# Three blocks of a gate projection written as seven-product blocks, with three engines kept in program order

## The chip, the cores and the metric

The kernel runs on one core of one Trainium2 chip. The metric is the time of one execution on the device in microseconds (us); a comparison takes the median of several runs. The engines of the core are TensorE (PE in the rows, with its weight load PEld), VectorE (DVE), ScalarE (ACT), GpSimd (POOL) and SyncE (SP), whose queue issues nearly all transfers.

## What is computed

One layer of a hybrid decoder: 512 tokens, width 1024, float32. A windowed attention (A) and a gated linear attention (B) run on the same normalised input `h`, and their projections are merged through two gates. Then follow a SwiGLU feed-forward part, a gated per-layer input and a final norm. The part that matters here:

```python
h = rms_norm(x, norm_mix)
proj = h @ w_in                       # q, k, v, ..., og, gate_a, gate_g side by side
o_g = rms_norm(o_g, gla_norm) * silu(og)
y_g = o_g @ w_proj_gla
mixed = sigmoid(gate_a) * y_a + sigmoid(gate_g) * y_g
x = x + mixed @ w_out
```

`gate_g = h @ w_in[:, 4880:5904]` is the merge gate of the linear attention: 1024 columns, worked on in four blocks of 256, called `gg0` to `gg3` in the kernel. The next matrix after it is `w_proj_gla`, the blocks `pg0` to `pg3`.

## The kernel before

**Arithmetic.** Every float32 operand of a large product is split into a high and a low part (`split`, L105): ScalarE casts the high part (L111), VectorE subtracts it from the source for the low part (L112). `mm3` (L121) then makes one float32 product out of three matmuls, high by high, high by low and low by high (L122 to L124). That is why each product stands under three lines in the rows.

**Two ways to make a block of 256 weight columns by 512 tokens.** The plain one is `fm_pair`: two halves of 128 columns (`e`), eight slices of the inner dimension, three matmuls each, every one 512 tokens wide: 48 matmuls. The other is `quad_pair`: the block is cut in two along columns, tokens and inner dimension, and sums of quarter blocks replace one of the eight quarter products, so there are seven. Each is four slices by three matmuls of 256 tokens: 84 matmuls. It needs sums of the tokens' side (`h_t1` to `h_t4`, made once and kept), and for each block two sums of the weights, made by `sums_to`: one VectorE operation of 128x1024 (`s0`) and two GpSimd operations of 128x512 (`s1`), all at L253. Its products run as follows: `pa`, `pb`, `pa` again, `pc`, `pa`, `pb`, `pa`. The bank `pa` accumulates over four of the seven, and after each of these ScalarE copies its present value out (`copy`, L580: `u` twice, `v`, then the second half of the result); the next product on `pa` has to wait for that copy. VectorE adds the other banks to the copies (`add`, L576). The kernel uses `quad_pair` for most of q/k (`qk1` to `qk3`), for the output gate `og0` to `og3` and for the whole feed-forward input (`fg..`, `fu..`).

**Weights.** `Weights` holds the order of all weight tiles. Raw weights come in by SyncE's queue (L243) into a ring of four half tiles, that is two whole ones (`RAW = 4`); the feed-forward weights have one whole tile more. One block of 256 columns fills one whole tile. The load for a block is issued when the block two before it has given its raw tile back: a plain block does that when both halves are split, a seven-product block after its last split (`.3`) and its sums. `take` splits two tiles ahead (`AHEAD = 2`) and makes sums up to `SUMS = 5` tiles ahead.

**Order.** Each engine executes its list strictly in the order of the built program, and SyncE issues its transfers likewise. The lists are made by a scheduler with priorities, except in sections under `tc.manual_schedule`, where the engines named there keep the order in which the code was written. Before the change such sections are the start of the kernel and the feed-forward part. Transfers that are not weights go through `aside` (L309), which puts them on SyncE's queue behind the last weight load that the code has asked for by then.

**Around the gate.** While `gg0` runs, the last head of the linear attention ends on the other engines (`lin`); its result goes to DRAM in eight pieces (`ogd`, L311). `og_splits` loads it back in two transfers of 1 MB (`ogr0` with rows 0 to 3, `ogr1` with rows 4 to 7) and splits each in two halves into `og_h`, `og_l`, the operand of `pg0`. The tanh of each gate block (L1080) goes to DRAM as `mgd` and comes back as `mg` when `pg` is evacuated. All of `gg1` to `gg3`, the splits of `ogr` and the weights of `pg` are in lists that the scheduler made.

Of the kernel before, what the change touches and what calls it, by code (L numbers as in the profile page):

```python
# [20 lines left out]
KD = D // P  # L21
# [7 lines left out]
C_GK, C_OG, C_GA, C_GG = 2816, 2832, 3856, 4880  # L29
# [4 lines left out]
def hybrid_layer(  # L34
# [26 lines left out]
    nc = tc.nc  # L61
# [18 lines left out]
    def tok(t):  # L80
        return slice(t * P, (t + 1) * P)

    def a8(name, shape=(P, 4, S), dt=F32):
        return big.tile(list(shape), dt, tag="a8", name=name)

    def t2(name, shape=(P, 512), dt=F32):
        return tp.tile(list(shape), dt, tag="t2", name=name)

    def bank(name):
        return psum.tile([P, 512], F32, tag="ps", name=name)  # L90
# [17 lines left out]
    def split(dst, src, scale=None, eng=nc.vector):  # L108
        hi, lo = dst
        if scale is None:  # L110
            ins = nc.scalar.copy(hi, src)  # L111
            eng.tensor_tensor(out=lo, in0=src, in1=hi.bitcast(F32), op=ALU.subtract)  # L112
        else:
            ins = nc.scalar.activation(hi, src, AF.Copy, scale=scale)  # L114
            nc.vector.scalar_tensor_tensor(  # L115
                out=lo, in0=src, scalar=scale, in1=hi.bitcast(F32), op0=ALU.mult, op1=ALU.subtract
            )
        return ins.ins

    def mm3(ps, l, r, first, last, more=False):  # L120
        kw = dict(skip_group_check=True) if more else {}  # L121
        nc.tensor.matmul(ps, lhsT=l[0], rhs=r[0], start=first, stop=False, **kw)  # L122
        nc.tensor.matmul(ps, lhsT=l[0], rhs=r[1], start=False, stop=False, **kw)  # L123
        nc.tensor.matmul(ps, lhsT=l[1], rhs=r[0], start=False, stop=last, **kw)  # L124


    wk = w_in.rearrange("(k p) c -> p k c", p=P)
# [10 lines left out]
    def u_quad(name, mat, c0):  # L138

        units.append((name, None, [[((ALL,), mat[:, 4 * kh : 4 * kh + 4, c0 : c0 + 256])] for kh in range(2)]))  # L140

    def u_rows(name, mat, k0, n, c0, ncol=512, per=2):

        for u in range(n // per):
            k = k0 + per * u
            units.append((f"{name}{u}", (per, ncol), [((ALL,), mat[:, k : k + per, c0 : c0 + ncol])]))
# [28 lines left out]
    for i in range(4):  # L175
# [5 lines left out]
                [((slice(64 * g, 64 * g + 64),), wpa[g][:, :, 256 * i : 256 * i + 256]) for g in range(2)],  # L181
            )
        )
    for i in range(4):
        u_rows(f"gg{i}", wk, 0, KD, C_GG + 256 * i, 256, 4)
    for i in range(4):
        u_rows(f"pg{i}", wpg, 0, KD, 256 * i, 256, 4)
    for i in range(2):
# [117 lines left out]
    W = Weights()  # L306

    def aside(dst, src):

        with tc.issue_after(W.dma.ins):  # L310
            nc.sync.dma_start(dst, src)  # L311
# [67 lines left out]
    for i in range(2):  # L379
        ps = bank(f"gm{i}")  # L380
# [25 lines left out]
    hT = HQuads("h")  # L406
# [63 lines left out]
    for t in range(NT):  # L470
        ps = bank(f"v0ps{t}")
# [73 lines left out]
    def fm_mms(ps, w, cols, rhs, k0, nk, first, last):  # L545
        for k in range(nk):
            mm3(ps, (w[0][:, k, cols], w[1][:, k, cols]), rhs.rows(k0 + k), first and k == 0, last and k == nk - 1)

    def flush(late, every=False):

        for job in late or []:
            job[0] -= 1
        while late and (every or min(late)[0] < 1):
            late.pop(late.index(min(late)))[2]()

    def quad_pair(name, act, c, evac, late=None):


        def done(e):
            if late is None:  # L560
                evac(e)
            else:
                late.extend(evac(e))

        pa, pb, pc = (bank(f"{name}p{x}") for x in "abc")
        H = (slice(0, 256), slice(256, 512))

        def product(ps, w, i, x, first=True):
            hi, lo = act.q(x)
            for k in range(4):  # L570
                mm3(ps, (w[0][:, i, k, :], w[1][:, i, k, :]), (hi[:, k, :], lo[:, k, :]), first and k == 0, k == 3, not first)


        def add(out, a, b):
            with tc.high_priority(offset=1000):
                nc.vector.tensor_tensor(out=out, in0=a, in1=b, op=ALU.add)  # L576

        def copy(out, a):
            with tc.high_priority(offset=1000):
                nc.scalar.copy(out, a)  # L580


        part = t2(f"{name}u"), t2(f"{name}v")
        p1, u2, u3, u4 = (part[i // 2][:, H[i % 2]] for i in range(4))
        run = pa[:, H[0]]
        w = W.take(f"{name}.0")
        product(run, w, 0, "b11")
        copy(p1, run)
        flush(late)
        product(pb[:, H[0]], w, 1, "b21")  # L590
        add(c[0][:, H[0]], pb[:, H[0]], p1)
        yield
        w = W.take(f"{name}.1")
        product(run, w, 0, "t2", False)
        copy(u2, run)
        flush(late)
        product(pc[:, H[0]], w, 1, "b22")
        add(u4, pc[:, H[0]], u2)
        yield
        w = W.take(f"{name}.2")  # L600
        product(run, w, 0, "t3", False)
        copy(u3, run)
        flush(late)
        product(pb[:, H[1]], w, 1, "t1")
        add(c[0][:, H[1]], pb[:, H[1]], u4)
        done(0)
        add(c[1][:, H[1]], pb[:, H[1]], u3)
        yield
        w = W.take(f"{name}.3")
        product(run, w, 0, "t4", False)  # L610
        copy(c[1][:, H[0]], run)
        flush(late)
        done(1)
        yield

    def fm_pair(name, act, evac):

        pss = [bank(f"{name}p{x}") for x in "ab"]
        for kh in range(2):
            w = W.take(f"{name}{kh}")  # L620
            for e in range(2):
                fm_mms(pss[e], w, tok(e), act, 4 * kh, 4, kh == 0, kh == 1)
                if kh:
                    evac(e, pss[e])
                yield

    def drive(stream, other=None, rate=1):
        for _ in stream:
            if other is not None:
                for _ in range(rate):  # L630
                    next(other, None)
# [4 lines left out]
    ps = bank("bias_ps")  # L636
# [411 lines left out]
    def times_gate(out, t, y, eng=nc.vector):  # L1048
        eng.scalar_tensor_tensor(out=out, in0=t, scalar=1.0, in1=y, op0=ALU.add, op1=ALU.mult)
# [22 lines left out]

    mx = Split("mx")

    def gates_g():
        for i in range(4):
            c = [t2(f"sgg{i}{e}") for e in range(2)]

            def evac(e, ps):
                nc.scalar.activation(c[e], ps, AF.Tanh, scale=0.5)  # L1080
                aside(mgd[i, 1, e], c[e])

            yield from fm_pair(f"gg{i}", hT, evac)

    def og_splits():
        for i in range(2):
            o = a8(f"ogr{i}")
            aside(o, ogd[4 * i : 4 * i + 4].rearrange("k p t -> p k t"))
            for h in range(2):
                ks_ = slice(2 * h, 2 * h + 2)  # L1090
                split(ogT.part(i, ks_, ALL), o[:, ks_, :])
                yield

    gg = gates_g()
    for _ in range(4):
        next(gg)
        next(lin, None)
    for _ in lin:
        pass
    ogT = Split("og")  # L1100
    ogs = og_splits()
    drive(gg, ogs)
    for _ in ogs:
        pass
    for i in range(4):
        mg = a8(f"mg{i}", (P, 2, 2, 512))
        for m in range(2):
# [1 line left out]
        c = [t2(f"yg{i}{e}") for e in range(2)]  # L1109

        def evac(e, ps):
            times_gate(c[e], mg[:, 1, e], ps)
            nc.vector.tensor_tensor(out=c[e], in0=c[e], in1=mg[:, 0, e], op=ALU.add)
            split(mx.rows(2 * i + e), c[e])
# [153 lines left out]
    for gi, (f0, nf) in enumerate(FFN):  # L1268
        act = Split(f"act{gi}", nf)

        def inner():
            for i in range(nf // 2):
                gs = [t2(f"g{gi}{i}{e}") for e in range(2)]
                us = []

                def silu(e, gs=gs):
                    yield [1, next(jobs), lambda: nc.scalar.activation(gs[e], gs[e], AF.Silu)]

                def mult(e, i=i, gs=gs, us=us):
                    yield [  # L1280
                        1 + e,
                        next(jobs),
                        lambda: nc.vector.tensor_tensor(out=us[e], in0=us[e], in1=gs[e], op=ALU.mult),  # L1283
                    ]
                    yield [3, next(jobs), lambda: split(act.rows(2 * i + e), us[e])]

                yield from quad_pair(f"fg{gi}{i}", h2.hT, gs, silu, late)
                us += [t2(f"u{gi}{i}{e}") for e in range(2)]
                yield from quad_pair(f"fu{gi}{i}", h2.hT, us, mult, late)
# [8 lines left out]
        stream, late, jobs = inner(), [], count()  # L1298
# [117 lines left out]
```

## Time and profile before

| | |
|---|---|
| time, median of 3 runs | 871.7 us (871.03 to 872.21) |
| the profiled execution: time | 872.2 us |
| the profiled execution: span of the core | 870.4 us |
| TensorE busy in the span | 854.0 us, 98% |
| VectorE / ScalarE / GpSimd busy | 565.7 / 446.2 / 160.8 us |
| mean granted TensorE clock | 0.998 of full speed |
| `gg1`, first matmul, to `pg0`, first matmul | 332.84 to 365.48 us |

Times inside the kernel are us from the start of the span. The profiled execution is 0.5 us above the median of the runs and its span 1.8 us shorter than its time. Starts of matmuls are recorded; their ends are modelled, so distances between starts are what counts on TensorE.

### The profile page before, as it was taken

What the parts mean: (1) busy time and instruction counts of PE and PEld (TensorE: products, weight loads), DVE (VectorE), ACT (ScalarE), POOL (GpSimd) and SP (SyncE); (2) the same over time, 40 slices, a digit from 0 to 9 for tenths busy, and PEclk for the clock granted to TensorE, in tenths of its full rate; (3) what the DMA queues carried; (4) which work ended last, traced back from release to release, by engine and by line L of the source; (5) the groups of instructions that cost most, each with busy time, mean ns of one, the idle gap of its engine ahead of it and who ended that gap; (6) DMA issues with size and microseconds to landing.
All of it is one profiled execution on the core that took longest, in us unless ns stands there. A gap on an engine that the chain in (4) does not pass through costs nothing. (4 is left out here: it accounts for less than half of the span.)

```text
span 870.4 us, 14739 instructions
## 1 busy us (share of the span) xinstructions
PE 854.0 (98%) x5901; PEld 748.7 (86%) x5901; DVE 565.7 (65%) x821; ACT 446.2 (51%) x859; POOL 160.8 (18%) x149
## 2 busy tenths in 40 slices
PE   8999989999999999999999999999999999999996
PEld 7977878888777788888887999889999889998886
DVE  5533866769876643356368799635998437985574
ACT  6336587866755543333256556413565314554453
POOL 4340434120221110100011222011232012210101
PEclk9999999999999999999999999999999999999999
DMA  9382423133764256774415233611316311422502
GB/s 282 103 215 78 152 74 97 50 102 102 236 206 158 74 170 216 271 265 146 142 54 164 94 126 108 232 49 49 95 52 211 129 49 49 136 87 94 194 1 98
DMA packets 88245, 113.29 MB, mean 130 GB/s; under 512 B 6152, under 2 KB 64304, under 8 KB 87792
## 3 DMA queue, kind: packets, MB, share of 16 engines
q1 hardware_dynamic: 86704, 107.43, 38.2%
q0 software_dynamic: 1456, 4.92, 1.6%
q8 instruction: 46, 0.75, 0.4%
q14 instruction: 23, 0.19, 0.1%
q10 hardware_dynamic: 16, 0.00, 0.0%
HBM read 95.35 MB, written 15.93 MB: 128 GB/s over the span
## 5 line engine op out<-in xcount | busy, mean ns | idle before, releaser
L111 ACT CAST fo_h<-raw 128x1024 fp32r<-128x1024 f32 x22 | 22.5, 1050 | 30.5 <-PE fo00ps L124 13.1
L112 DVE TENSOR_TENSOR fo_l<-raw,fo_h 128x1024 fp32r<-128x1024 f32 x22 | 26.3, 1220 | 12.1 <-ACT fo_h L111 12.1
L326 POOL TENSOR_TENSOR or<-om,mhalf 128x1 f32<-128x1 f32 x16 | 14.2, 886 | 68.1 <-DVE om L330 54.2
L112 DVE TENSOR_TENSOR act_l<-u,act_h 128x512 fp32r<-128x512 f32 x22 | 22.1, 1004 | 5.4 <-ACT act_h L111 5.4
L905 DVE TENSOR_TENSOR zs<-zs,kq 128x512 f32<-128x512 f32 x28 | 19.5, 707 | 7.0 <-ACT zs L901 6.3
L112 DVE TENSOR_TENSOR pg_l<-raw,pg_h 128x1024 fp32r<-128x1024 f32 x8 | 9.8, 1223 | 18.5 <-ACT pg_h L111 18.5
L112 DVE TENSOR_TENSOR wo_l<-raw,wo_h 128x1024 fp32r<-128x1024 f32 x8 | 9.8, 1224 | 17.7 <-ACT wo_h L111 17.7
L115 DVE SCALAR_TENSOR_TENSOR gt_l<-raw,gple,gt_h 128x256 fp32r<-128x256 f32 (+1 forms) x24 | 12.9, 570 | 12.0 <-ACT gt_h L114 11.9
L114 ACT ACTIVATE gt_h<-raw,gple 128x256 fp32r<-128x256 f32 (+1 forms) x24 | 12.6, 573 | 12.4 <-PE gt0ps L124 8.1
L111 ACT CAST act_h<-u 128x512 fp32r<-128x512 f32 x22 | 13.7, 622 | 10.0 <-DVE u L1283 10.0
L111 ACT CAST wo_h<-raw 128x1024 fp32r<-128x1024 f32 x8 | 8.4, 1053 | 20.1 <-PE wo0ps L124 6.6
L112 DVE TENSOR_TENSOR gg_l<-raw,gg_h 128x1024 fp32r<-128x1024 f32 x8 | 9.8, 1224 | 12.9 <-ACT gg_h L111 12.9
L899 DVE TENSOR_TENSOR zs<-G 128x512 f32<-128x512 f32 x24 | 16.1, 692 | 2.4 <-DMA G<-Gd 2.4
L111 ACT CAST pg_h<-raw 128x1024 fp32r<-128x1024 f32 x8 | 8.4, 1055 | 15.7 <-PE gg3pb L123 5.8
L112 DVE TENSOR_TENSOR v_l<-raw,v_h 128x1024 fp32r<-128x1024 f32 (+1 forms) x8 | 9.3, 1167 | 11.1 <-ACT v_h L111 11.1
L997 ACT ACTIVATE own<-o,or 128x256 f32<-128x256 f32 x16 | 7.6, 475 | 17.1 <-POOL or L326 16.9
L1283 DVE TENSOR_TENSOR u<-u,g 128x512 f32<-128x512 f32 x22 | 16.1, 733 | 0.0
L111 ACT CAST v_h<-raw 128x1024 fp32r<-128x1024 f32 (+1 forms) x10 | 9.6, 973 | 11.9 <-PE v2ps L124 4.5
L792 ACT ACTIVATE s_all<-s_all,nm 128x256 f32<-128x256 f32 (+1 forms) x32 | 15.2, 480 | 0.7 <-DVE nm L789 0.7
L112 POOL TENSOR_TENSOR qa<-qa,qs 64x768 fp32r<-64x768 f32 x2 | 7.2, 3616 | 41.6 <-ACT qs L111 41.5
L111 ACT CAST gg_h<-raw 128x1024 fp32r<-128x1024 f32 x8 | 8.4, 1049 | 12.2 <-PE ga3pb L123 4.2
L112 DVE TENSOR_TENSOR qa_l<-raw,qa_h 128x512 fp32r<-128x512 f32 x8 | 5.5, 719 | 13.2 <-ACT qa_h L111 13.2
(2312 smaller groups left out, 3550.1 us busy)
## 6 DMA issues: line engine op xcount, KB each, us to landing
raw<-in_w_ffn_in SPq DMA_DIRECT2D x44, 512.0 KB, 4.7
raw<-in_w_in SPq DMA_DIRECT2D x39, 512.0 KB, 4.7
raw<-in_w_ffn_out SPq DMA_DIRECT2D x22, 512.0 KB, 4.8
raw<-in_w_proj_gla SPq DMA_DIRECT2D x8, 512.0 KB, 5.7
mg<-mgd SPq DMA_DIRECT2D x8, 512.0 KB, 7.0
raw<-in_w_out SPq DMA_DIRECT2D x8, 512.0 KB, 4.5
raw<-in_w_ple_gate SPq DMA_DIRECT2D x8, 512.0 KB, 4.3
raw<-in_w_in SPq DMA_DIRECT2D x8, 256.0 KB, 5.0
```

The costliest lines, as they stand in the source:

```text
L111: ins = nc.scalar.copy(hi, src)
L112: eng.tensor_tensor(out=lo, in0=src, in1=hi.bitcast(F32), op=ALU.subtract)
L114: ins = nc.scalar.activation(hi, src, AF.Copy, scale=scale)
L115: nc.vector.scalar_tensor_tensor(out=lo, in0=src, scalar=scale, in1=hi.bitcast(F32), op0=ALU.mult, op1=ALU.subtract)
L326: return r, nc.gpsimd.tensor_tensor(out=r, in0=a, in1=mhalf, op=ALU.pow)
L792: nc.scalar.activation(s[:, a, :], s[:, a, :], AF.Exp, bias=nm[:, a : a + 1], accum_out=su[:, a : a + 1])
L899: pe.tensor_tensor(out=z3, in0=g3, in1=g3[:, :, b - 1 : b].broadcast_to([P, nb, 2 * b]), op=ALU.subtract)
L905: nc.vector.tensor_tensor(out=d4, in0=d4, in1=kq_, op=ALU.mult)
L997: nc.scalar.activation(v_[:, c, :], po[:, 0:256], AF.Copy, scale=r)
L1283: lambda: nc.vector.tensor_tensor(out=us[e], in0=us[e], in1=gs[e], op=ALU.mult),
```

## The change

`gg1`, `gg2` and `gg3` become seven-product blocks; `gg0` stays plain. Their tanh is made in place on the finished tile, as a job that is put off by one product (`late`, `flush`). The rest of the stage, from the first product of `gg1` on, stands under `manual_schedule` for ScalarE, VectorE and GpSimd, with six places written by hand for `og_splits`: load `ogr0` after step 0, its two splits after steps 3 and 5, load `ogr1` after step 6, its splits after steps 9 and 11 (a block has four steps). TensorE's and SyncE's lists are still the scheduler's. `SUMS` is 4 in the section.

```diff
-    for i in range(4):
-        u_rows(f"gg{i}", wk, 0, KD, C_GG + 256 * i, 256, 4)
+    u_rows("gg0", wk, 0, KD, C_GG, 256, 4)
+    for i in range(1, 4):
+        u_quad(f"gg{i}", wk, C_GG + 256 * i)
...
+    late, jobs = [], count()
+
     def gates_g():
         for i in range(4):
             c = [t2(f"sgg{i}{e}") for e in range(2)]
 
-            def evac(e, ps):
+            def evac(e, ps, c=c, i=i):
                 nc.scalar.activation(c[e], ps, AF.Tanh, scale=0.5)
                 aside(mgd[i, 1, e], c[e])
 
-            yield from fm_pair(f"gg{i}", hT, evac)
+            def tanh(e, c=c, evac=evac):
+                yield [1, next(jobs), lambda: evac(e, c[e])]
+
+            if i:
+                yield from quad_pair(f"gg{i}", hT, c, tanh, late)
+            else:
+                yield from fm_pair(f"gg{i}", hT, evac)
...
             aside(o, ogd[4 * i : 4 * i + 4].rearrange("k p t -> p k t"))
+            yield
             for h in range(2):
...
-    drive(gg, ogs)
-    for _ in ogs:
-        pass
+
+    W.SUMS = 4
+    with tc.manual_schedule(engines={nc.scalar.engine, nc.vector.engine, nc.gpsimd.engine}):
+        for n, _ in enumerate(gg):
+            if n in (0, 3, 5, 6, 9, 11):
+                next(ogs)
+        flush(late, True)
+    W.SUMS = 5
```

SyncE's list from the last weights of the gate to the loads for `pg` (`raw25` is the whole tile of `gg3`, `raw26` of `pg0`, `raw27` of `pg1`, each loaded in two halves). Before:

```order
L243 DMA raw25_3613<-in_w_in 128x4x256 x2
L311 DMA mgd_1971<-sgg00_3605 128x512
L311 DMA ogd_1967<-og6_3673 128x512
L311 DMA ogd_1967<-og7_3681 128x512
L311 DMA mgd_1971<-sgg01_3606 128x512
L243 DMA raw26_3710<-in_w_proj_gla 128x4x256
L311 DMA ogr0_3724<-ogd_1967 128x4x512
L243 DMA raw26_3710<-in_w_proj_gla 128x4x256
L311 DMA mgd_1971<-sgg10_3702 128x512
L311 DMA ogr1_3761<-ogd_1967 128x4x512
L311 DMA mgd_1971<-sgg11_3703 128x512
L243 DMA raw27_3789<-in_w_proj_gla 128x4x256 x2
```

The same stretch of SyncE's list after the change:

```order
L244 DMA raw25_3618<-in_w_in 128x4x256
L312 DMA mgd_1971<-sgg00_3610 128x512
L312 DMA ogd_1967<-og6_3682 128x512
L312 DMA ogd_1967<-og7_3690 128x512
L312 DMA mgd_1971<-sgg01_3611 128x512
L312 DMA ogr0_3750<-ogd_1967 128x4x512
L244 DMA raw25_3618<-in_w_in 128x4x256
L244 DMA raw26_3787<-in_w_proj_gla 128x4x256
L312 DMA mgd_1971<-sgg10_3713 128x512
L312 DMA mgd_1971<-sgg11_3714 128x512
L244 DMA raw26_3787<-in_w_proj_gla 128x4x256
L244 DMA raw27_3918<-in_w_proj_gla 128x4x256
L312 DMA ogr1_3947<-ogd_1967 128x4x512
```

The first half of `raw25` now waits for VectorE's last split of `gg1` (`gg1.3_l`), the first half of `raw26` for that of `gg2`, the first half of `raw27` for that of `gg3` (`gg3.3_l`). `ogr1`, which stood ahead of `raw27`, stands behind it.

ScalarE's list at the end of the gate, where the seven copies, the casts of `og` and those of `pg` meet. Before:

```order
L1080 ACTIVATE sgg11_3703<-gg1pb_3705 128x512
L111 CAST og_h1_3699<-ogr1_3761 128x1024 x2
L111 CAST pg00_h_3852<-raw26_3710 128x1024
L1080 ACTIVATE sgg20_3781<-gg2pa_3783 128x512
L111 CAST pg01_h_3882<-raw26_3710 128x1024
L1080 ACTIVATE sgg21_3782<-gg2pb_3784 128x512
L111 CAST pg10_h_3922<-raw27_3789 128x1024
L1080 ACTIVATE sgg30_3848<-gg3pa_3850 128x512
```

ScalarE's list there after the change:

```order
L111 CAST gg3.3_h_4007<-raw25_3618 128x512
L581 COPY gg3u_3973<-gg3pa_3970 128x256
L111 CAST og_h1_3708<-ogr1_3947 128x1024
L111 CAST pg00_h_4039<-raw26_3787 128x1024
L581 COPY gg3v_3974<-gg3pa_3970 128x256
L111 CAST pg01_h_4073<-raw26_3787 128x1024
L111 CAST pg10_h_4105<-raw27_3918 128x1024
L111 CAST pg11_h_4135<-raw27_3918 128x1024
L581 COPY sgg31_3969<-gg3pa_3970 128x256
L1083 ACTIVATE sgg30_3968<-sgg30_3968 128x512
L111 CAST og_h1_3708<-ogr1_3947 128x1024
```

The first cast of `ogr1` now stands between the copies of `gg3` out of bank `pa`. One block earlier the first cast of `ogr0` stands in the same way ahead of the first copy of `gg2`:

```order
L1083 ACTIVATE sgg10_3713<-sgg10_3713 128x512
L111 CAST og_h0_3707<-ogr0_3750 128x1024
L111 CAST gg2.2_h_3844<-gg2.0s0_3658 128x1024
L581 COPY gg2u_3842<-gg2pa_3839 128x256
L1083 ACTIVATE sgg11_3714<-sgg11_3714 128x512
```

In TensorE's list `gg1` and `gg3` have the seven products in the order given above; in `gg2` the product on `pc` stands ahead of the second one on `pa`. One matmul of `pg0` stands ahead of the last product of `gg3`.

## Rows read from the trace of the kernel before

**Rows 1.** TensorE's waits in the whole span: us in total, times, longest us.
```profile
PE pt L806 <- ACT s_all L796: 2.4, 1, 2.4
```

**Rows 2.** TensorE's timeline: start us, us, operation; around the gate.
```profile
303.55 1.03 PE L1026 MATMUL ogt<-ident,own 128*128 128x128 f32 x8
...
332.84 0.39 PE L122 MATMUL gg1pa<-h_h,gg_h 128*128 128x512 f32 x1
...
365.48 0.39 PE L122 MATMUL pg0pa<-og_h,pg_h 128*128 128x512 f32 x1
```

**Rows 3.** TensorE's timeline, feed-forward part: a wait for a copy, two block starts.
```profile
485.46 0.28 PE L124 MATMUL fu00pc<-h_b,fu00.1_l 128*128 128x256 f32 x1
486.17 0.39 PE L122 MATMUL fu00pa<-h_t,fu00.1_h 128*128 128x256 f32 x1 [0.42 <-ACT fu00u L580]
...
522.76 0.28 PE L122 MATMUL fu02pa<-h_b,fu02.0_h 128*128 128x256 f32 x1
...
532.84 0.28 PE L122 MATMUL fg03pa<-h_b,fg03.0_h 128*128 128x256 f32 x1
```

**Rows 4.** ScalarE's timeline in the block fu02 of the feed-forward part.
```profile
525.59 0.61 ACT L111 CAST fu02.3_h<-raw 128x512 fp32r<-128x512 f32 x1
527.28 0.37 ACT L580 COPY fu02u<-fu02pa 128x256 f32<-128x256 f32 x1 [1.08 <-PE fu02pa L124]
```

**Rows 5.** VectorE's timeline in fu02 and fg12: sum, add, splits.
```profile
526.07 1.22 DVE L253 TENSOR_TENSOR fg03.0s<-raw 128x1024 f32<-128x1024 f32 x1
527.20 0.42 DVE L576 TENSOR_TENSOR u<-fu02pb,fu02u 128x256 f32<-128x256 f32 x1
...
529.53 1.98 DVE L112 TENSOR_TENSOR fg03.0_l<-raw,fg03.0_h 128x1024 fp32r<-128x1024 f32 x1
...
532.27 1.22 DVE L112 TENSOR_TENSOR fg03.1_l<-fg03.0s,fg03.1_h 128x1024 fp32r<-128x1024 f32 x1
...
641.03 0.68 DVE L112 TENSOR_TENSOR fg12.3_l<-raw,fg12.3_h 128x512 fp32r<-128x512 f32 x1
```

**Rows 6.** GpSimd's timeline: the head's `or` (om23's power), a second weight sum.
```profile
298.39 0.55 POOL L326 TENSOR_TENSOR or<-om,mhalf 128x1 f32<-128x1 f32 x1 [3.97 <-DVE om L330]
...
528.80 1.63 POOL L253 TENSOR_TENSOR fg03.0s<-raw,fg03.0s 128x512 f32<-128x512 f32 x1
```

**Rows 7.** SyncE's queue, timeline of issues around the gate.
```profile
330.63 0.98 SPq L311 DMA_DIRECT2D ogd<-og  x2
...
335.15 0.38 SPq L243 DMA_DIRECT2D raw<-in_w_proj_gla  x1
335.58 0.54 SPq L311 DMA_DIRECT2D ogr<-ogd  x1
...
342.32 1.07 SPq L311 DMA_DIRECT2D ogr<-ogd  x1
```

**Rows 8.** VectorE's timeline: the last split of gg2.
```profile
333.90 1.22 DVE L112 TENSOR_TENSOR gg_l<-raw,gg_h 128x1024 fp32r<-128x1024 f32 x1 [2.64 <-ACT gg_h L111]
```

**Rows 9.** ScalarE's timeline: a tanh, the casts of ogr0 and ogr1 (two each).
```profile
341.20 0.60 ACT L1080 ACTIVATE sgg<-gg1pa 128x512 f32<-128x512 f32 x1 [1.89 <-PE gg1pa L124]
342.07 2.00 ACT L111 CAST og_h<-ogr 128x1024 fp32r<-128x1024 f32 x2 [0.28 <-DMA ogr<-ogd]
...
348.46 2.00 ACT L111 CAST og_h<-ogr 128x1024 fp32r<-128x1024 f32 x2 [2.94 <-DMA ogr<-ogd]
```

**Rows 10.** Page, part 6: issues, KB each, median us from issue to landing.
```profile
mg<-mgd SPq DMA_DIRECT2D x8, 512.0 KB, 7.0
...
ogr<-ogd SPq DMA_DIRECT2D x2, 1024.0 KB, 6.3
```

**Rows 11.** Last stretches of the span: us, busy us (x) per engine, PEclk, DMA.
```profile
860.00:866.00 6.00, 2.61 (x22) 2.40 (x21) 3.61 (x10) 2.97 (x8) 1.49 (x3) 1.00 0.46 186
866.00:870.40 4.40, 0.00 (x0) 0.00 (x0) 0.55 (x1) 0.61 (x1) 0.14 (x1) 0.64 0.30 119
```

**Rows 12.** TensorE's timeline at the kernel's start: warm-up products, 512 wide.
```profile
6.56 1.89 PE L370 MATMUL idle<-ones 128*128 128x512 bf16 x4
```

## The prediction

> **What bounds the kernel now.** TensorE is busy 98% of the span, and its list of waits is short: the longest single one is 2.4 us, far from this stage [rows 1]. So the stage is to be read on TensorE first, then on whatever can make it wait. From the first product of gg1 to the first of pg0 go 32.64 us [rows 2], three blocks of 10.88 us, 48 matmuls each, 0.227 us from start to start, with no gap. The other engines have air there. The things to look at next are the rows of a seven-product block in the feed-forward part, where such blocks already run in program order [rows 3 to 6], and the queue of SyncE with the casts that wait for its transfers [rows 7 to 9], because the change moves just these against each other.
>
> **What the change saves on TensorE.** A seven-product block takes 532.84 - 522.76 = 10.08 us [rows 3]: 84 matmuls of 256 tokens, 0.12 us each, 1.44 us for one product of twelve. Against 10.88 us that is 0.80 us a block and **2.40 us** for three. This is the whole gain to be had, and it is there only if the products follow one another without a gap.
>
> **What it adds on the other engines.** Per block VectorE has three splits and a sum at 1.22, a half split at 0.68 and four adds at about 0.4 [rows 5]: 7.2 us in 10.08. Over the three blocks 21.6, with the four splits of og (4.9) and two for pg0 (2.4) 28.9 of 30.2 us. ScalarE has three casts of 1.05, one of 0.61, four copies of 0.37 and two tanh of 0.60 [rows 4, 9]: 6.4 us a block. GpSimd's two sums are at most 1.63 each [rows 6], and a VectorE split beside such a sum took 1.98 instead of 1.22 [rows 5]. The feed-forward blocks carry as much and keep to 10.08, so the work as such costs nothing; what hides it is the next 1.44 us product, and where that cover is gone a late copy costs its full length. Ahead of gg1 the sum for gg1 takes the place of the split of gg00 on VectorE, which goes behind `om23`, at equal length; GpSimd's two sums come before `or`, which began at 298.39 [rows 6]. Begun at that time at the latest they end 3.3 us later, at 301.7; `or` with 0.55 and ScalarE's own scaling, about half a us, end near 302.7, and the transposes that need them start at 303.55 [rows 2]. Cost nothing, with 0.8 us of cover; without it at most 1 us. The tanh is later by some us than its stores to DRAM need; they are read only by `mg` (below).
>
> **What it moves: the loads of og.** Before, the raw tile of gg1 was free long before gg1 ran, so the two halves of raw25 were already issued. Now a raw tile is free only after the `.3` split of its block, and SyncE, which issues strictly in its list's order, stands there with all that is behind. That it does so, rows 7 and 8 show: raw26 (335.15) went out when the last split of gg2 ended (333.90 + 1.22 = 335.12), and ogr0, whose data had long been in DRAM, only behind it at 335.58. From there to the cast at 342.07 are 6.4 us; for ogr1, 342.32 to 348.46, 6.1; the page's median is 6.3 [rows 9, 10].
>
> *gg2.* gg1 runs from 332.84 to 342.92. A copy or add starts 0.2 us behind its product: u of fu02's third product at 527.28 against 522.76 + 4.32 = 527.08 [rows 3, 4]. So the add for gg1's second product starts at 335.92, takes 0.42, and the split gg1.3_l follows with 0.68 [rows 5]: 337.0. Then SyncE issues half of raw25, four stores and ogr0; at some 0.45 us each [rows 7] ogr0 goes out at 339.2. With 6.3 us it lands at 345.5. By bytes it would be later: in before the two halves of raw26 and ogr0, 2 MB, were issued from 335.15 on and in by 342.0, 6.85 us; now raw25, four stores and ogr0 are 3 MB from 337.0 on, 10.3 us, 347.3. I take 346.0, nearer to the first, since the stores go to DRAM and the second half of raw25 stands behind ogr0. ScalarE in program order has the cast of og_h0, the cast gg2.2 and then the first copy of gg2; two casts stand 0.95 apart (2.00 for a pair [rows 9]), so the copy is done at 346.0 + 0.95 + 0.95 + 0.37 = 348.3. TensorE has meanwhile done the products on pa, pb and, by its order in gg2, pc, until 342.92 + 4.32 = 347.24. It waits 1.1 us. And since the two next products both go to pa, the copy between them lies bare: 485.46 to 486.17 is 0.71 instead of 0.12 [rows 3], **0.6** more. Stall in gg2: **1.7 us** (0.6 where ogr0 is in time, 3.0 at 347.3). gg3 starts at 342.92 + 10.08 + 1.7 = 354.7.
>
> *gg3.* Its split gg3.3_l comes at the same distance as in gg1, 4.2 us, plus some tenths because GpSimd's sums for gg3 run late and beside VectorE's splits: 359.2. SyncE then issues half of raw27, and ogr1 at 359.65. Landing 6.3 us later: 365.95. On ScalarE the cast of og_h1 stands behind the second copy of gg3, and behind it the cast of pg00 and the third copy: done at 365.95 + 0.95 + 0.95 + 0.37 = 368.2. TensorE's seventh product on pa needs that copy. The sixth ends at 354.7 + 8.64 = 363.34. Stall: **4.95 us** (with 5.0 us, which is ogr1 counted from the end of its issue, 343.39 to 348.4: 3.65; with 8.0, 6.4 scaled by the 2.5 MB that are queued together here against 2 MB then: 6.65). One matmul of pg0 stands ahead of the seventh product and runs in the gap, **-0.23**.
>
> *Behind it.* pg0 goes on at about 369.8, 4 us later than before, and needs the second half of og_h1 6.8 us after that. ScalarE's list has pg01, pg10, pg11 (which waits for the seventh product, 369.8), a copy, a tanh and that cast: 372.7, VectorE's split 374, before 376.5. Hidden by 2.5 us. The store of the last tanh is now behind that, and mg0 behind the store: issued at some 373.8, landing 7.0 later [rows 10], 380.8, where VectorE wants it at 378. VectorE waits 3 us; queued behind is the split pg21, which TensorE needs only in the second half of pg2, 15 us later. Nothing. From pg1 on the list is as before and every engine is later by the same amount.
>
> **The sum**: -2.40 + 1.7 + 4.95 - 0.23 = **+4.0 us** (+1.6 to +7.0). Made against the profiled execution it gives 872.2 + 4.0 = 876.2; that one lies 0.5 above the median of the runs, so the forecast is 871.7 + 4.0 = **875.7 us** (873.3 to 878.7).
>
> **Rivals.** *The loads come in time.* For the seventh product of gg3 to go on at once its copy must be done at 363.4, ogr1 landed at 361.1, so issued at 354.8, five us earlier than I read it. That would be so if raw27 did not wait for gg3.3_l, or if a landing took a us. Then only gg2's stall is left: 871.7 - 2.4 + 1.7 = 871.0, no difference; if ogr0 too is in time, 871.7 - 2.4 = **869.3**, faster. The point from which the sign turns is a stall of 2.4 in both together. For it: the feed-forward part runs such blocks without a gap. Against: that part has no cast of a late transfer in ScalarE's list and one raw tile more.
>
> *The gap costs the clock.* The gap in gg3 is 4.8 us from start to start (363.2 to 368). In this trace the granted clock stayed full over 2.4 us [rows 1]; behind the last product, which ended at 862.6 (2.61 busy from 860), it was full until 866 and 0.64 on average in the last 4.4 us [rows 11]; falling from 1 to a half, it fell near 867.2, 4.6 us after TensorE stopped. My gap is as long, so it can go either way. [...] How long it would stay there behind a gap no row shows; I take 4 us, about what the fall took, which cost 2 us: **877.7**; twice that with a longer spell.
> [...]
>
> *VectorE becomes the bound.* 28.9 of 30.2 us leave little, and beside GpSimd's sums a split takes 0.76 more. Three such blocks could add about 1 us to the stalls; it is within the range.
>
> **How the numbers follow.** Forecast 0.58; the clock 0.20; only the stall in gg2, or stalls of about the gain, 0.12; no stall 0.10. About 0.2%, 1.7 us, is what a measurement of this kernel can tell from no change. The first two are slower, 0.78; the third is the same, 0.12; the last faster, 0.10. The range 872.4 to 879.4 leaves out the last, part of the third and the longest cold spells.
>
> **What would show it.** In the profile after: products of 0.12 us in gg1 to gg3 and gg1 in 10.08; ScalarE's waits should have a DMA of ogr ahead of og_h of 1 to 2 us in gg2 and about 6 in gg3; TensorE a wait of about 5 us for the copy gg3v, 1 us and 0.6 for gg2u; SyncE's ogr1 within 1 us behind gg3.3_l. Wrong it would be if ogr1 went out before gg3.3_l, if the landing took under 3 us, or if a product waited for a split of weights instead.

## The result, and the profile after

The changed kernel takes 881.98 us (median of four runs, 880.46 to 882.50) against 871.44: a ratio of 1.0112, 95% interval 1.01 to 1.0125 (the two medians alone give 1.0121). It is slower, as forecast, but by 10.5 us instead of 4.0, and outside the range. The profiled execution has a span of 880.3 us, 9.9 more than before.

TensorE's waits between 325 and 400 us (which line and tile, what it waited for, us in total, times, longest) are at two places; the kernel before has none there:

```profile
PE pg0pa L122 <- ACT pg_h L111: 5.5, 1, 5.5
PE gg2pa L122 <- ACT gg2u L581: 4.0, 2, 3.5
```

The first is charged to pg0's cast because one matmul of pg0 stands ahead of gg3's seventh product; that product waits at the same place, for the copy gg3v. On TensorE's timeline (start, duration of one, tile, in brackets the idle time before it and its releaser), first gg2, then gg3:

```profile
346.87 0.28 PE L124 MATMUL gg2pc<-h_h,gg2.1_l 128*128 128x256 f32 x1
350.64 0.39 PE L122 MATMUL gg2pa<-h_t,gg2.1_h 128*128 128x256 f32 x1 [3.50 <-ACT gg2u L581]
...
366.97 0.28 PE L124 MATMUL gg3pb<-h_t,gg3.2_l 128*128 128x256 f32 x1
372.72 0.80 PE L122 MATMUL pg0pa<-og_h,pg_h 128*128 128x512 f32 x1 [5.47 <-ACT pg_h L111]
373.32 0.41 PE L122 MATMUL gg3pa<-h_t,gg3.3_h 128*128 128x256 f32 x1
```

What stands on ScalarE ahead of the copies that TensorE needs, in the same columns:

```profile
348.33 1.04 ACT L111 CAST og_h<-ogr 128x1024 fp32r<-128x1024 f32 x1 [4.56 <-DMA ogr<-ogd]
349.28 1.04 ACT L111 CAST gg2.2_h<-gg2.0s 128x1024 fp32r<-128x1024 f32 x1
350.23 0.36 ACT L581 COPY gg2u<-gg2pa 128x256 f32<-128x256 f32 x1
...
370.68 1.04 ACT L111 CAST og_h<-ogr 128x1024 fp32r<-128x1024 f32 x1 [7.34 <-DMA ogr<-ogd]
371.63 1.04 ACT L111 CAST pg_h<-raw 128x1024 fp32r<-128x1024 f32 x1
372.58 0.36 ACT L581 COPY gg3v<-gg3pa 128x256 f32<-128x256 f32 x1
```

ScalarE idles 4.6 and 7.3 us for the two og loads, with a cast and then the copy that TensorE needs behind the waiting cast. SyncE's issues (start, time for the group, destination and source), and the VectorE split that SyncE waits for in the second group:

```profile
336.83 0.38 SPq L244 DMA_DIRECT2D raw<-in_w_in  x1
337.26 0.73 SPq L312 DMA_DIRECT2D mgd<-sgg  x1
338.05 0.97 SPq L312 DMA_DIRECT2D ogd<-og  x2
339.06 0.79 SPq L312 DMA_DIRECT2D mgd<-sgg  x1
339.95 0.78 SPq L312 DMA_DIRECT2D ogr<-ogd  x1
340.77 0.71 SPq L244 DMA_DIRECT2D raw<-in_w_in  x1
...
356.38 6.75 SPq L244 DMA_DIRECT2D raw<-in_w_proj_gla  x2
363.23 0.45 SPq L312 DMA_DIRECT2D ogr<-ogd  x1
...
362.00 0.68 DVE L112 TENSOR_TENSOR gg3.3_l<-raw,gg3.3_h 128x512 fp32r<-128x512 f32 x1
```

In the kernel before, ogr0 was issued at 335.58 and ogr1 at 342.32 [rows 7]; now 339.95 and 363.23. The second stands behind raw27a, the first half of raw27 (in the group of two that takes 6.75 us), which waits for the last split of raw25: it ends at 362.00 + 0.68.

Last, the clock that TensorE was granted. Some stretches of 1 us with, per engine from PE to POOL, the busy time and the number of instructions, then PEclk, DMA share, GB/s:

```profile
350.00:351.00 1.00, 0.35 (x3) 0.36 (x4) 1.00 (x2) 1.00 (x3) 0.00 (x0) 1.00 0.00 0
351.00:352.00 1.00, 1.00 (x10) 1.00 (x9) 1.00 (x2) 0.63 (x2) 0.00 (x0) 0.92 0.00 0
352.00:353.00 1.00, 0.63 (x3) 0.34 (x2) 1.00 (x2) 0.33 (x2) 0.00 (x0) 0.50 0.00 0
...
354.00:355.00 1.00, 1.00 (x7) 1.00 (x7) 1.00 (x2) 0.94 (x1) 0.92 (x2) 0.50 0.00 0
355.00:356.00 1.00, 1.00 (x9) 1.00 (x9) 1.00 (x2) 0.22 (x1) 1.00 (x1) 0.87 0.01 3
...
371.00:372.00 1.00, 0.00 (x0) 0.00 (x0) 0.24 (x1) 1.00 (x2) 0.00 (x0) 1.00 1.10 439
...
373.00:374.00 1.00, 1.00 (x5) 0.96 (x6) 1.00 (x1) 1.00 (x2) 0.00 (x0) 0.50 1.04 414
...
375.00:376.00 1.00, 1.00 (x7) 1.00 (x6) 1.00 (x2) 0.00 (x0) 0.00 (x0) 0.63 1.03 408
```

At either gap the granted clock falls to 0.50 for some 3.4 us (352 to 355 and a part of the stretch on either side; 373 to 375 and such parts). At the first gap it fell at 351.8, when TensorE had been working again since 350.64; at the second at 372.3, before the first matmul. The kernel before had 1.00 throughout 332 to 386 us.

**The account.** The first matmul of pg1 moved from 376.36 (365.48 + 10.88 [rows 2]) to 386.67, +10.3 us. From the changed kernel's timeline: gg1 begins 0.24 us earlier (332.60). Three blocks of seven save 2.40. gg2 loses 3.65 at its first copy (3.77 from start to start, less the 0.12 of a matmul) and 0.75 at its second, 4.40 together; the rest of its 15.78 us over 10.08 + 4.40 is slow matmuls, 1.30. gg3's seventh product starts 6.23 us after its sixth has ended (366.97 + 0.12). From it to pg1 are 13.35 us against 12.09 at full clock, 1.26. One pg0 matmul lies in the gap, -0.23. Sum: -0.24 - 2.40 + 4.40 + 1.30 + 6.23 + 1.26 - 0.23 = **+10.3**. (The spans differ by 9.9; the 0.4 between lies behind 466 us, outside this stage.)

### The profile page after: what moved, and what is told of

Its sections match the earlier page's. It is cut to its first block, busy times and chain, and to the rows that moved or that the text cites. A ratio compares the mean times of both kernels' runs of the same rounds, so it can differ in the third digit from the quotient of the medians.

```text
span 880.3 us, 15019 instructions
## 1 busy us (share of the span) xinstructions
PE 855.1 (97%) x6009; PEld 754.5 (86%) x6009; DVE 580.9 (66%) x842; ACT 453.5 (52%) x877; POOL 170.4 (19%) x155
## 5 line engine op out<-in xcount | busy, mean ns | idle before, releaser
L112 DVE TENSOR_TENSOR og_l<-ogr,og_h 128x1024 fp32r<-128x1024 f32 x4 | 5.6, 1412 | 13.5 <-ACT og_h L111 13.5
L111 ACT CAST mx_h<-yg 128x512 fp32r<-128x512 f32 x8 | 5.0, 622 | 18.4 <-DVE yg L1128 18.4
L1292 ACT ACTIVATE g<-g 128x512 f32<-128x512 f32 x22 | 14.0, 634 | 0.0
L797 ACT ACTIVATE s_all<-s_all,rd 128x256 f32<-128x256 f32 (+1 forms) x32 | 13.2, 478 | 1.1 <-DVE rd L795 1.1
```

The lines of the kernel that those rows point to most:

```text
L797: nc.scalar.activation(s[:, a, :w], s[:, a, :w], AF.Copy, scale=rd[:, a : a + 1])
```

## The experiments

All edits are to the changed kernel. Theory A is the prediction's mechanism: copies queue behind casts that wait for og loads, the loads are late because SyncE holds them behind weight loads, and the clock falls in the gaps. Its rivals are named in each expectation. The kernel before, measured beside these runs, took 871.7 to 872.3 us; each ratio is against it.

**Casts moved behind the copies, one half at a time, then both.** The steps at which the load and the two splits of each half are written:

```
-            if n in (0, 3, 5, 6, 9, 11):
-                next(ogs)
+            for _ in range((0, 6, 6, 6, 9, 11).count(n)):   # e1_late0
+            for _ in range((0, 3, 5, 6).count(n)):          # e2_late1, the rest behind flush
+            for _ in range((0, 6, 6, 6).count(n)):          # e3_late01, the rest behind flush
+                next(ogs)
```

> The casts and splits of the first loaded half of og (ogr0) stand behind the block gg2's third copy on ScalarE and VectorE, not ahead of its first; everything else as in the changed kernel. Theory A (the copies of TensorE's banks queue behind casts that wait for the og loads, and TensorE's clock falls in the gaps): gg2's gaps of 3.8 and 0.9 us close and its matmuls run at full clock, -4.4 -1.3 us; gg3 keeps its gap of about 5.5 us, since its load is held behind raw27a, which moves with gg2. 876.3 us (875 to 877.5). Theory B (the load lands when it lands; the wait only moves to the next reader): 880 to 882 us. Theory C (the seven-product blocks or the program order itself cost the time on VectorE and GpSimd): 881 to 883 us, no change.

> The casts and splits of the second loaded half of og (ogr1) stand behind gg3's last copy and last tanh; ogr0's stay where the changed kernel has them. Theory A: gg3's gap of 5.5 us closes (the seventh product starts 6.2 us earlier) and pg0 runs at full clock, about -1.3 us more; og's second half is first wanted by pg0's second half, some 7 us after gg3's sixth product, when a load that lands 3.7 us after that product is ready. 874.5 us (873.5 to 876). gg2 keeps its gaps. Theory B (the wait only moves to pg0): 879 to 882 us. Theory C: 881 to 883 us.

> Both edits of the two runs before: ogr0's casts behind gg2's third copy, ogr1's behind gg3's last. Theory A: the two stalls add up, 882.0 - 5.7 - 7.5 = 868.8 us (868 to 871), faster than the kernel before by about the 2.4 us that three blocks of seven products save. Theory B: 878 to 882 us. Theory C: 881 to 883 us.

Measured: e1_late0 880.45 us (ratio 1.0097, 1.0082 to 1.0112), e2_late1 874.64 (1.0027, 1.0015 to 1.0039), e3_late01 871.96 (0.9997, 0.9987 to 1.0007).

e2 is what theory A asked for: gg3's wait is gone and 7.3 us with it; pg0 follows without a gap, so the wait does not move on to it. e1 is not: its time lies in the range of theory B. gg2 does run without a gap (343.0 to 353.2), but gg3 takes longer. The longest of TensorE's waits, ScalarE's cast of ogr1, and the clock behind it:

```profile
PE pg0pa L122 <- ACT pg_h L111: 6.1, 1, 6.1
...
367.89 1.04 ACT L111 CAST og_h<-ogr 128x1024 fp32r<-128x1024 f32 x1 [7.86 <-DMA ogr<-ogd]
...
371.00:372.00 1.00, 1.00 (x6) 1.00 (x6) 1.00 (x4) 1.00 (x2) 0.00 (x0) 0.50 1.06 420
...
374.00:375.00 1.00, 1.00 (x4) 0.81 (x3) 0.26 (x1) 0.00 (x0) 0.11 (x1) 0.50 1.05 323
```

gg3 began 5.2 us earlier than in the changed kernel, but ogr1 was issued only 2.5 us earlier (360.72) and landed only 2.8 earlier (367.89 against 370.68). SyncE waits for gg3's last split, and that ended 7.0 us after gg3's start instead of 4.2, because VectorE had waited 2.35 us for raw25b, the second half of raw25, and had both of ogr0's splits to do in between. And the clock was at 0.50 for some 6.8 us instead of 3.4. So it is not ogr0's wait that moved, as theory B has it, but a second load that stayed late: of the 5.5 us that gg2 gave back, 2.5 went into a longer way to gg3's seventh product and 1.0 into slow matmuls behind it. Closing the first gap alone paid 1.5 us of the 5.7 expected. e3, with both closed, is 1 us above theory A's range. TensorE has small waits left there that are VectorE's, and VectorE itself had waited for a load:

```profile
PE gg2pb L122 <- DVE sgg L577: 1.3, 1, 1.3
PE gg3pa L124 <- DVE gg3.1_l L112: 0.8, 1, 0.8
PE gg3pa L124 <- DVE gg3.0_l L112: 0.5, 1, 0.5
...
349.58 1.22 DVE L254 TENSOR_TENSOR gg3.0s<-raw 128x1024 f32<-128x1024 f32 x1 [3.74 <-DMA raw<-in_w_in]
```

The sum for gg3 waits for raw25b, issued at 340.93 behind ogr0 and in at 349.5. In VectorE's program order gg2's add stands behind that sum. So there was a third late load beneath the two, which cost nothing as long as gg2 stood still.

**The clock alone.** TensorE is given work that nobody reads, in the gaps:

```
+        def spin(n):
+            hi, _ = act.q("b11")
+            for _ in range(n):
+                nc.tensor.matmul(pc[:, H[1]], lhsT=w[0][:, 0, 0, :], rhs=hi[:, 0, :], start=True, stop=True)
...
+        if name == "gg2":
+            spin(28)
         product(run, w, 0, "t2", False)
...
         product(pb[:, H[1]], w, 1, "t1")
+        if name == "gg3":
+            spin(44)
```

> The changed kernel with 28 matmuls of 128x256 without use in gg2's gap (some 3.3 us, into a quarter of a bank that nobody reads) and 44 (some 5.2 us) in gg3's, so that TensorE works while it waits; the waits themselves stay. Theory A1 (the fallen clock behind the gaps is 2.5 to 3 us of the loss): granted clock 1.00 from 343 to 386 us and 879.0 us (878.3 to 880). Theory A2 (the waits are the whole loss; the matmuls behind the gaps are slow for another reason): 882 us or more, 881.5 to 883.

Measured: 879.94 us (1.0085, 1.0068 to 1.0102), 2.0 less than the changed kernel, within A1. The clock was kept up:

```profile
343.00:354.00 11.00, 9.82 (x82) 9.62 (x81) 5.30 (x6) 5.66 (x10) 0.80 (x1) 1.00 0.46 160
354.00:358.00 4.00, 4.00 (x36) 4.00 (x35) 4.00 (x4) 2.24 (x3) 2.12 (x2) 1.00 0.40 100
370.00:374.00 4.00, 3.90 (x33) 3.70 (x32) 2.74 (x4) 3.82 (x5) 1.04 (x2) 1.00 1.06 408
374.00:378.00 4.00, 4.00 (x20) 3.31 (x19) 2.55 (x3) 1.36 (x3) 0.53 (x1) 1.00 1.04 398
```

So the fallen clock is about 2 us of the loss (2.56 in the account), and the rest is waiting, 10.6 us less the 2.4 saved. The 2 are not exact: the edit also moved TensorE's list. The product on pc now stands behind the gap in gg2, which is 4.70 us long from start to start instead of 4.40 for two, and the gap in gg3 is 5.54 without the matmul of pg0 instead of 6.23 with it.

**The loads made early, casts left ahead of the copies.** Three ways: GpSimd's queue (e5_pool), another buffer for raw25, so that SyncE need not wait (e6_far3), and both og loads right behind raw25a on SyncE (e9_early). In e5 and e9 both loads are asked for at step 0, and the four splits stay at steps 3, 5, 9 and 11.

```
 # e5_pool; e9_early has aside(...) in place of nc.gpsimd.dma_start(...)
+        os_ = [a8(f"ogr{i}") for i in range(2)]
+        for i, o in enumerate(os_):
+            nc.gpsimd.dma_start(o, ogd[4 * i : 4 * i + 4].rearrange("k p t -> p k t"))
 # e6_far3
+                if n % 2 == 0 and self.loads[n] and self.loads[n][0][:3] in ('gg3',):
+                    self.whole.append(a8(f"raw{n // 2}", (P, 2, 1024)))
```

> Both og loads are issued on GpSimd's own queue instead of SyncE's, the second at the end of gg2's sums, so that no weight load that waits for a split stands ahead of them; all casts stay in the places of the changed kernel, ahead of the copies. Theory A (the copies wait because the og loads are late, held behind weight loads and sharing the transfer time with raw25b): both are in place when their casts come, and raw25b lands some 3 us sooner; no gap over 1 us in gg2 and gg3: 868.8 us (868 to 870.5). Theory D (with the late loads gone VectorE is the bound in gg2 and gg3, as in the kernel with both casts late, where its sum for gg3 and its splits held TensorE 1.3, 0.5 and 0.8 us): 871 to 872.5 us. Theory B (casts ahead of copies cost by their place, landed or not): 875 us or more.

> gg3's weights (raw25) load into a buffer of the large pool instead of one of the two that take turns, so raw25 needn't wait for gg1's last split, nor raw27 for gg3's, but for gg2's; SyncE then reaches ogr0 some 10 us earlier and ogr1 some 8 us earlier, without any change to the order of ScalarE, VectorE and GpSimd. Theory A: as with the og loads on GpSimd's queue, both stalls go, and gg3's sums find raw25 loaded: 868.8 us (868 to 870.5). Theory D (VectorE bound): 870.5 to 872.5 us. Theory E (the buffer of the large pool comes free too late, and the loads for gg1 stand behind it): over 875 us with a new gap in gg1.

> Both og loads stay on SyncE's queue but stand together right behind raw25a, ogr1 no longer behind raw27a; casts and copies as in the changed kernel. Theory A: ogr0 is issued where it was, so gg2's gap of 3.8 us stays, or grows by up to 1 us since another 1 MB shares the transfer time; ogr1 is loaded some 10 us before its casts, so gg3's gap and its clock go (-6.2 -1.3 us); raw25b, now behind both, lands up to 2.5 us later and may hold gg3's sum. 875.5 us (874 to 878). Theory G (it is the load's size and the shared transfer time alone that make ogr1 late, not the place in the queue): over 879 us.

Measured: e5_pool 869.95 us (0.9983, 0.9973 to 0.9992), e6_far3 869.98 (0.9979, 0.9969 to 0.9988), e9_early 875.60 (1.0042, 1.0029 to 1.0056). With the casts where they were, ahead of the copies, the loss turns into a gain as soon as the loads are in, so theory B falls (in e6 raw25 too comes early). Theory D falls but for 0.3 us. In e6 the og loads are issued at 296.6 and 351.14; the one wait left to TensorE there:

```profile
351.14 0.42 SPq L314 DMA_DIRECT2D ogr<-ogd  x1
...
PE gg3pa L124 <- DVE gg3.0_l L112: 0.3, 1, 0.3
```

e9 has ogr1 early and ogr0 where it was, keeps gg2's gap (3.8 us) and loses gg3's, and theory A's time is met to a tenth. Theory G falls: not the size of the load but its place in SyncE's queue made ogr1 late.

**Each half of the change alone.** Blocks of eight products in program order (e7_pairs), and blocks of seven with the three engines left to the scheduler (e8_sched):

```
 # e7_pairs
-    u_rows("gg0", wk, 0, KD, C_GG, 256, 4)
-    for i in range(1, 4):
-        u_quad(f"gg{i}", wk, C_GG + 256 * i)
+    for i in range(4):
+        u_rows(f"gg{i}", wk, 0, KD, C_GG + 256 * i, 256, 4)
...
 # e8_sched
-    with tc.manual_schedule(engines={nc.scalar.engine, nc.vector.engine, nc.gpsimd.engine}):
+    with nullcontext():
```

> The program order alone: all four blocks of the gate as they were before (eight products), but the last three in program order on ScalarE, VectorE and GpSimd, with the og loads and casts at the changed kernel's steps. Theory A (the order hurts only through copies of a bank that TensorE needs at once, and blocks of eight products have none): 871.5 us (870.8 to 873), the casts' waits hidden. Theory C (the program order itself costs): 875 us or more.

> The seven-product blocks alone: the three engines are ordered by the scheduler again. In its order the first cast of og_h0 still stands right ahead of gg2's first copy, but those of og_h1 behind gg3's third. Theory A: gg2 keeps its gap (4 us and 1.3 of clock), gg3's closes: about 874.6 us (873.5 to 876), near the kernel with only ogr1's casts late. Theory C (the program order is the loss, seven products are fine): 868.5 to 870 us. Theory F (seven products cost as such): 880 us or more.

Measured: e7_pairs 871.50 us (0.9998, 0.9989 to 1.0008), e8_sched 872.81 (1.0015, 1.0005 to 1.0025). Program order alone costs nothing that can be measured: in e7 ScalarE sat 2.59 us for ogr1 at 357.99 and TensorE waited for nothing. In e8 theory A was right that gg3 has no wait, and 1.8 us too high, below its range. ogr0 went out at 337.27 there, 2.7 us earlier, and cost gg2 0.4 us at its first copy instead of 3.5. A longer wait of 2.3 us stands at the third copy, gg2v, and it is not og's. ScalarE:

```profile
353.38 1.04 ACT L111 CAST gg3.1_h<-gg3.0s 128x1024 fp32r<-128x1024 f32 x1 [4.30 <-POOL gg3.0s L254]
354.33 0.37 ACT L581 COPY gg2v<-gg2pa 128x256 f32<-128x256 f32 x1
```

The scheduler put a cast of gg3's weight sum ahead of that copy, and the sum was late: GpSimd's second half of it ran from 351.22 to 353.35. So that theory A named gg2 is in part luck; the pattern is the same, with a sum in place of a load. At these shorter gaps the granted clock stayed 1.00. Theory C, which wanted the seven-product blocks to gain under the scheduler, falls too.

**Both cures, and the fourth block.** e10_far3late is e6 with the steps (0, 5, 6, 6, 10, 11); e11_all4 is e6 with gg0 in seven products as well.

> gg3's weights in a buffer of the large pool, and besides the casts of ogr0 behind gg2's second and third copy and those of ogr1 behind gg3's. If the 0.5 us that gg3 still loses comes from ScalarE's or VectorE's order (og's splits ahead of gg3's): 869.4 us (868.8 to 870). If VectorE's work as a whole is the bound there, 870.0 us, no change (869.5 to 870.8).

> gg3's weights in a buffer of the large pool, and the first block gg0 in seven products too. If gg0 has its inputs in time, another 0.8 us less: 869.2 us (868.6 to 870). If its loads or VectorE, which serves the linear attention's last chunks beside it, hold it: 870 to 873 us.

Measured: e10_far3late **868.98 us** (0.9966, 0.9953 to 0.9979), the fastest of all; e11_all4 870.88 (0.9995, 0.9986 to 1.0004). First matmuls of each block in e10 (four of one kind, first and last start):

```profile
L122 PE MATMUL gg1pa<-h_h,gg1.0_h x4: 278/283/283, 332.4 to 333.5; 128*128 128x256 f32 x4
L122 PE MATMUL gg2pa<-h_h,gg2.0_h x4: 283/283/283, 342.5 to 343.6; 128*128 128x256 f32 x4
L122 PE MATMUL gg3pa<-h_h,gg3.0_h x4: 283/283/283, 352.6 to 353.7; 128*128 128x256 f32 x4
L122 PE MATMUL pg0pa<-og_h,pg_h x8: 389/389/396, 362.7 to 370.2; 128*128 128x512 f32 x8
```

10.1 us a block three times, as in gg1 of the changed kernel. So VectorE's work as a whole is not the bound; in e6 it was the place of og's split ahead of gg3's. (By the two profiles e10 gains 0.75 us on e6 between gg1 and pg1; gg1 also begins 0.5 earlier there, which the edit does not explain.) e11 does not gain on e6, and gg0 is not worth it as it stands; where its 0.8 us went I did not follow further (TensorE's waits there name 0.6 us for the linear attention's last transposes and 0.3 for gg0's first copy).

## Why the prediction was wrong in size

The mechanism was right and three terms of the sum were too small, by 6.5 us together: gg2's stall 4.40 us for 1.7, gg3's 6.23 for 4.95, and the clock, which the sum put at nothing, 2.56; gg1's earlier start takes 0.24 off. (The stalls in the sum stand some 0.07 us above their own terms, too little to matter.)

**Right.** A block is 10.08 us (gg1 10.07, e10 10.1 each). gg1 begins 0.24 us early, so no loss ahead of it shows; in the runs above it begins anywhere from 331.9 to 333.9, so a loss below 1 us could hide there. (One GpSimd sum ahead of it took 2.14 us, above the 1.63 that I had as the most.) SyncE holds ogr0 behind raw25a and ogr1 behind raw27a: issued 0.75 us later than I had it for ogr0, and 4.78 us after gg3's start for ogr1 against 4.95 forecast. The casts stand in ScalarE's list where I read them, and the waits came at the two copies I named; ScalarE sat idle for 4.6 and 7.3 us with ready work behind, so there it kept strictly to the order of its list. Behind pg0 the list was harmless: VectorE waited 6.8 us for mg0 instead of 3, and TensorE for nothing.

**The term that failed first: the landing of ogr0.** I took 346.0, between 345.5 by the durations of before and 347.3 by bytes; it landed at 348.3, 8.4 us after its issue instead of 6.3 [rows 10], beyond my upper end. The transfers in the changed kernel:

```profile
336.00:338.00 2.00, 2.00 (x19) 2.00 (x19) 0.76 (x2) 0.89 (x2) 0.00 (x0) 1.00 0.12 18
338.00:346.00 8.00, 8.00 (x69) 8.00 (x68) 3.44 (x5) 2.65 (x5) 0.00 (x0) 1.00 0.98 338
346.00:348.00 2.00, 1.15 (x10) 0.94 (x8) 0.00 (x0) 0.00 (x0) 0.00 (x0) 1.00 0.51 182
```

From the issue of raw25a on, 3 MB are on their way. Nearly nothing moves in the first 1.2 us (why stays open); then the transfer engines are full for 8 us, and by 348.0 the rows add up to 3.1 MB, which is all of it, stores and raw25b too. A median taken where a load shares the engines with 1 MB is no price where it shares them with 2. I had the better figure in hand (by bytes) and leaned to the other, on the argument that the stores and raw25b do not count. By these rows they do, though no run takes them away alone. e9_early, with the same list ahead of ogr0 and ogr1 behind it as well, agrees: 8.6 us (341.42 to 349.99). The first wait became 3.65 us instead of 1.1; with the second copy (0.75 for 0.6) gg2's stall is 4.40 for 1.7.

**The second: the landing of ogr1**, 7.4 us instead of 6.3, beside raw27b and x's four rows (2 MB) on GpSimd's queue: the transfer engines' share is 0.92 to 1.04 in each us from 367 to the landing. In e7_pairs, where x's rows are issued only at 359.57, ogr1 landed 5.8 us after its issue. gg3's stall is 6.23 us for 4.95, inside the bound of 6.65.

**The third: the clock**, left to a rival with a chance of 0.20 and to one gap. It fell at both, also at the one of 3.5 us, and cost 1.3 + 1.26 us in the account and about 2.0 by e4_spin. I took 2 us for one spell, which is too much (1.3), and missed that a longer stall elsewhere brings a second. Those 2 us were my estimate: no row ahead of the prediction shows how fast work goes on while the granted clock is down, for the four products of rows 12 ran at a listed 1.00. In the changed kernel, at a granted 0.50, a matmul of 256 tokens took 0.21 us from start to start (five from 353.90 to 354.97) instead of 0.12, and in e1_late0 one of 512 some 0.4 (373.1 to 373.5) instead of 0.23. The two falls also came at different times: in gg3 the clock was at 0.50 when TensorE went on, in gg2 the burst began at 1.00 and the clock fell 1.2 us later.

The errors have one sign, and in part they hang together: both loads land later beside more bytes, and at the longer gaps the clock fell. My range took both loads at their latest (878.7) but the clock only on the middle (877.7), not the two together: 871.7 - 2.4 + 3.0 + 6.65 - 0.23 + 2 is 880.7. The time is 1.3 above even that: gg2's stall passed its bound of 3.0, and there was a second spell.

**The rivals.** "The loads come in time" was the wrong case for this kernel but right in price: 869.3 forecast, 868.98 in e10, where they do. "VectorE becomes the bound", priced at about 1 us, is what e3 showed (2.6 us of waits), once the og waits were gone, and only by its order and raw25b: in e10 TensorE has no wait from gg1 to pg1.

## What to carry to other kernels

A change that holds a buffer longer delays its next load, and on a queue that issues in order, as SyncE's did here, everything written behind that load (ogr1 went out at 363.23 instead of 342.32); look at what else uses the queue before counting the products saved. Where an engine runs in program order, a step that waits for a transfer belongs behind the copies that free another engine's banks (here casts of loads, in e8_sched a cast of a late sum), and closing one such wait may pay little (1.5 us here for the first) until the next is gone too. Price a load by the bytes that are in flight beside it (ogr0 took 8.4 us beside 2 MB, against a median of 6.3 beside 1), and reckon with the fallen clock at every long wait of TensorE that the forecast itself creates: here it fell at all five of 3.1 to 6.1 us.

## What the runs showed of the hardware that I had not expected

The spell at a granted 0.50 did not go by the length of the gap. In gg2 of the changed kernel the clock was full until TensorE had worked again for over 1 us (350.64 to 351.8) and then low for the 3.4 us named above, and so it was in e9_early with a gap of 3.8 us (at work from 352.30, low from 353.4, 3.4 us). In e2_late1, with a gap of 3.1 us instead of 3.5 at the same place, it fell at 348.8, before TensorE resumed at 349.99:

```profile
348.00:349.00 1.00, 0.00 (x0) 0.00 (x0) 0.24 (x1) 1.00 (x2) 0.00 (x0) 0.90 0.06 20
349.00:350.00 1.00, 0.01 (x1) 0.01 (x1) 1.00 (x2) 1.00 (x3) 0.00 (x0) 0.50 0.00 0
...
354.00:355.00 1.00, 1.00 (x6) 1.00 (x6) 1.00 (x3) 1.00 (x2) 1.00 (x1) 0.50 0.00 0
355.00:356.00 1.00, 1.00 (x8) 1.00 (x7) 1.00 (x1) 0.22 (x1) 0.36 (x1) 0.69 0.41 80
```

and was low for about 6.8 us (six whole stretches from 349 on and parts of two), so that gg2 took 16.4 us there against 15.78 with the longer gap. The gap of 6.1 us in e1_late0 also had a spell of 6.8, that of 5.5 in the changed kernel one of 3.4. Behind gaps of 2.3 us (e8_sched) and 2.4 us [rows 1] it stayed at 1.00 (346 to 356 us, and 108 to 124 in the kernel before).
